# First projections of a decoder block: PSUM tiles that leave are summed over four K tiles, and low parts of weights stand behind the modulation sums in VectorE's order

## The chip, the cores and the metric

The kernel runs on one core of one Trainium2 chip. The metric is the device time of one execution in microseconds (us); the median of three runs before the change is 3016.16 us. TensorE is PE in the profile, VectorE DVE, ScalarE ACT, GpSimd POOL, and SyncE, which issues most DMAs, SP.

## The reference, cut to what matters

```python
D_MODEL = 2048; SEQ = 512            # one sequence, one layer
mod = c_act @ w_ada + b_ada          # c_act = silu(c): one row of 2048; w_ada: 2048 x 12288
sh1, sc1, gt1, sh2, sc2, gt2 = jnp.split(mod, 6, axis=-1)
h = modulate(rms_norm(x, g_mix), sh1, sc1)        # h * (1 + sc1) + sh1
z = h @ w_in
(q_sb, k_sb, v_sb, q_ds, k_ds, v_ds, q_ix, k_ix, w_ix,
 gate_sb, gate_ds) = split_columns(z)
...                                  # two attention branches, gates, w_out, a conv-gated FFN, a final norm
```

All is float32. The kernel computes a float32 product as three products of rounded parts: a factor a is split into a high part (ScalarE rounds it) and a low part (a minus the high part, on VectorE), and high x high, high x low and low x high are summed in PSUM.

## The kernel before, in words

The change lies in the first stage, from about 23 to 246 us. The rows of h are 16 K tiles of 128. Tile d of h needs columns d of the vectors sh1 and sc1, and each of these is a sum over all 2048 rows of w_ada, so that 4 MB of w_ada have to pass before two tiles of h can be made. The 16 K tiles are therefore taken in nine groups (`GR`, L45: one tile, seven times two, one). While PE multiplies group g with the weights, VectorE sums the columns of w_ada for group g + 1 and beyond.

**The modulation sums.** `first_ada` (L682) is a generator; one step is one item: 256 KB of w_ada, loaded by `first_load` (L288, SP) up to ten items ahead. In a group of two tiles there are 16 items, each one row block of 128 x 512. Nearly all are added by VectorE into one accumulator (L697 the first, L699 the others, each reads the accumulator that the one before wrote). In the groups after the second, two of the 16 go to PE instead (L679, `ON_PE`). When the items are through, `hidden` (L707) lets PE sum the accumulator over its partitions (L679 with a vector of ones), VectorE writes the vectors (L716 `modv`, L718 `smix`), and ScalarE makes two instructions per tile: the high part of h (L723) and the whole value (L729). `hidden_rest_` (L736) makes the low part on VectorE (L739).

**The products.** In each group four weight loads ("units") are used, in the order `ORD`: 512 columns of the indexer's queries, the 80 columns of the indexer's keys and weights, 512 more columns of the queries, and 512 columns of the first heads' q and k. A unit's K tiles are those of its group. Of the 13 PSUM tiles, five stay in PSUM through all nine groups (the queries 0, 1, 4, 5 and "kw"). The other eight leave after each group: `evac` (L750) copies the tile to SBUF on ScalarE (L752), and from the second group on VectorE adds it to what is there (L756).

**The order.** The order of the instructions on each engine is written out by hand: it is the order in which the Python code emits them. A unit is one entry of `steps`; before a unit runs, `ahead` (L233) loads weights up to five units on (four buffers) and calls `convert` (L219) for the unit two further on: ScalarE rounds (L229), VectorE subtracts (L230), at once. Then `first_go` (L758) emits the products of each PSUM tile, and after each tile `paced` (L785) emits up to three items of the modulation sums, towards a goal that runs ten items (`LEAD`) ahead of the next group; the goal is held at the end of the next group's sums until `hidden` of that group has been emitted. `hidden` of the next group stands before the third of the four units, `hidden_rest_` before the fourth. After each unit VectorE may get two products `xr` (L670, x times the row factor), and SP a spill of x to HBM.

Of the kernel before, what the change touches and what calls it, by code (L numbers as in the profile page):

```python
# [11 lines left out]
F32 = mybir.dt.float32  # L12
# [17 lines left out]
C_QSB, C_KSB, C_VSB = 0, 1024, 2048  # L30
C_QDS, C_KDS, C_VDS = 3072, 4096, 5120
C_QIX, C_KIX, C_GSB, C_GDS = 6144, 7168, 7248, 9296
# [6 lines left out]
AHEAD = 20  # L39
LEAD = 10  # L40
AHEAD = 10
OF = 2
SP0 = 22
ORD = (0,2,1,3)
GR = (1,2,2,2,2,2,2,2,1)  # L45
PLAIN = 4
DELAY = 3
# [40 lines left out]
SC0 = 4  # L88
LS = 8
L0 = 1  # L90
OF2 = 1
BY_DMA = 14


# [11 lines left out]
def block_kernel(ctx, tc, x, c, w_ada, b_ada, g_mix, w_in, w_o_sb, w_o_dsa, w_out, rel_bias,  # L106
                 g_ffn, w_gate, w_up, conv_w, conv_b, w_down, g_final, buckets, out, dbg=None):
    nc = tc.nc
    x, w_ada, w_in, w_o_sb, w_o_dsa, w_out = x[0], w_ada[0], w_in[0], w_o_sb[0], w_o_dsa[0], w_out[0]
# [18 lines left out]
    def ps():  # L128
        return psum.tile([128, 512], F32, tag="ps", name="ps")
# [11 lines left out]
    def U(w, k0, nk, c0, nn, fn, early=False):  # L141
        steps.append(((w, k0, nk, c0, nn, early), fn))
        units.append(steps[-1][0])
# [9 lines left out]
    def F(fn):  # L153
        steps.append((None, fn))
# [19 lines left out]
    def seven_blocks(r, spec):  # L174
# [3 lines left out]
        return (r.rearrange("p (q b c) -> p q b c", q=q, b=7),  # L178
                w[128 * k0:128 * (k0 + nk), c0:c0 + nn].rearrange("(q k p) (u c) -> p q k u c", q=q, p=128, u=2))

    def is_seven(spec):
        return isinstance(spec[5], str)

    def load(spec):
        w, k0, nk, c0, nn, kind = spec
# [16 lines left out]
    def loaded_sums(r, spec):  # L202

        if spec[5] == "seven by dma":
            b, wb = seven_blocks(r, spec)
            for u in range(2):
                nc.gpsimd.dma_start(b[:, :, 2 + u], wb[:, :, u, 1 - u], accum_op=OP.add)  # L207

    def sums_of(r, spec):

        if not is_seven(spec):
            return
        b, _ = seven_blocks(r, spec)
        if spec[5] == "seven":
            nc.vector.tensor_add(b[:, :, 2:4], b[:, :, 5:7], b[:, :, 0:1].to_broadcast([128, 2, 2, 128]))  # L215
        nc.vector.tensor_add(b[:, :, 1], b[:, :, 3], b[:, :, 5])  # L216
        nc.vector.tensor_add(b[:, :, 0], b[:, :, 4], b[:, :, 1])  # L217

    def convert(r, spec):  # L219

        nn, kind = spec[4], spec[5]
        h = wsp.tile([128, 1792], F32R, tag="wh", name="wh")
        l = wsp.tile([128, 1792], F32R, tag="wl", name="wl")
        if is_seven(spec):
            nc.scalar.copy(h, r)  # L225
            nc.vector.tensor_sub(l, r, h.bitcast(F32))  # L226
            return tuple(v.rearrange("p (q b c) -> p q b c", q=spec[2] // 2, b=7) for v in (h, l))
        h, l = h[:, 0:r.shape[1]], l[:, 0:r.shape[1]]
        nc.scalar.copy(h, r)  # L229
        (nc.gpsimd if kind else nc.vector).tensor_sub(l, r, h.bitcast(F32))  # L230
        return h.rearrange("p (k n) -> p k n", n=nn), l.rearrange("p (k n) -> p k n", n=nn)

    def ahead():  # L233

        def loads(n):
            while len(raws) < min(n, len(units)):
                raws.append(load(units[len(raws)]))

        def sums(n):
            while len(summed_) < min(n, len(units)):  # L240
                k = len(summed_)
                sums_of(raws[k], units[k])
                summed_.append(k)

        while len(parts) < min(at[0] + 3, len(units)):
            n = len(parts)
            loads(n + 4)
            while len(added_) < min(n + 3, len(units)):
                loaded_sums(raws[len(added_)], units[len(added_)])
                added_.append(True)  # L250
            sums(n + 2)
            parts.append(convert(raws[n], units[n]))
            raws[n] = None
# [28 lines left out]
    GROUPS = [(sum(GR[:i]), sum(GR[:i + 1])) for i in range(len(GR))]  # L282
# [424 lines left out]
    def hidden(k0, k1):  # L707

        while not fin:
            advance(back)  # L710
        p, acc, first = fin.pop(0)
        while late:
            evac(*late.pop())
        n = k1 - k0
        on_pe(p, acc, ones[:, 0:1], first, True)
        nc.vector.tensor_add(modv2[:, :, k0:k1], p[:, 0:2 * n].rearrange("p (v a) -> p v a", v=2),  # L716
                             vecs[:, 0:2 * KT].rearrange("p (v a) -> p v a", v=2)[:, :, k0:k1])
        nc.vector.scalar_tensor_tensor(smix[:, k0:k1], modv[:, SC1 * KT + k0:SC1 * KT + k1], 1.0,  # L718
                                       vecs[:, 96 + k0:96 + k1], op0=OP.add, op1=OP.mult)
        for d in range(k0, k1):  # L720
            s, b = smix[:, d:d + 1], modv[:, SH1 * KT + d:SH1 * KT + d + 1]
            h, l, u = T(F32R), T(F32R), xr[d]
            nc.scalar.activation(h, u, AF.Identity, scale=s, bias=b)  # L723
            if d == 0:
                y = T()
                nc.vector.tensor_scalar(y, u, s, b, op0=OP.mult, op1=OP.add)
                u = y
            else:
                nc.scalar.activation(u, u, AF.Identity, scale=s, bias=b)  # L729
            rest.append((l, u, h))  # L730
            xr[d] = None
            hT.append((h, l))
# [3 lines left out]
    def hidden_rest_():  # L736
        while rest:
            l, u, h = rest.pop(0)
            nc.vector.tensor_sub(l, u, h.bitcast(F32))  # L739

    FIRST = [(C_QIX, 512, [(2, 256, 128, False), (3, 384, 128, False), (0, 0, 128, True), (1, 128, 128, True)]),
             (C_QIX + 512, 512, [(6, 256, 128, False), (7, 384, 128, False), (4, 0, 128, True), (5, 128, 128, True)]),
             (C_KIX, 80, [("kw", 0, 80, True)]),
             ((C_QSB, C_KSB), 512, [("q0", 0, 128, False), ("q1", 128, 128, False), ("k0", 256, 128, False), ("k1", 384, 128, False)])]
    part, late = {}, []
    FIRST = [FIRST[i] for i in ORD]

    def evac(key, p, gi, w):  # L750
        t = T()
        nc.scalar.copy(t[0:w, :], p)  # L752
        if gi == 0:
            part[key] = t
        else:
            nc.vector.tensor_add(part[key], part[key], t)  # L756

    def first_go(h, l, gi, tiles):  # L758
        k0, k1 = GROUPS[gi]
        for key, off, w, stay in tiles:  # L760
            if not stay:
                p = ps()[0:w, :]
            elif gi == 0:
                p = part[key] = ps()[0:w, :]
            else:
                p = part[key]
            for k in range(k0, k1):
                mm3(p, h[:, k - k0, off:off + w], l[:, k - k0, off:off + w], *hT[k],
                    k == 0 if stay else k == k0, k == KT - 1 if stay else k == k1 - 1)
            if late:  # L770
                evac(*late.pop())
            if not stay:
                late.append((key, p, gi, w))
            paced(gi)

    def spill(d1):

        for d in range(len(xT_d), min(d1, len(xr))):
            xT_d.append(dram.tile([128, 512], F32, name=f"xT{d}"))
            nc.sync.dma_start(xT_d[d], xT[d])  # L780
            xT[d] = None

    steps_of = {}

    def paced(gi):  # L785

        if gi + 1 == len(GROUPS):
            return
        steps_of[gi] = steps_of.get(gi, 0) + 1
        goal = base[gi + 1] + LEAD + steps_of[gi] * (base[gi + 2] - base[gi + 1]) // sum(len(f[2]) for f in FIRST)  # L790
        if len(hT) < GROUPS[gi + 1][1]:
            goal = min(goal, base[gi + 2])
        for _ in range(3):
            if seen[0] < min(goal, base[-1]):
                advance(back)

    base = [sum(16 // (2 // (b - a)) for a, b in GROUPS[:g]) for g in range(len(GROUPS) + 1)]

    def start():
        nonlocal rate  # L800
        rate[0] = 0
        while len(raws) < 3:
            raws.append(load(units[len(raws)]))
        first_load(16)
        first_norm()
        scaled(1)
        back.append(first_ada())
        while not fin:
            advance(back)
        ahead()  # L810
        hidden(*GROUPS[0])
        hidden_rest_()

    F(start)
    for gi, (k0, k1) in enumerate(GROUPS):
        for i, (c0, nn, tiles) in enumerate(FIRST):
            if i == len(FIRST) - OF and gi + 1 < len(GROUPS):
                F(lambda g=gi + 1: hidden(*GROUPS[g]))
            if i == len(FIRST) - OF2:
                F(hidden_rest_)  # L820
            U(w_in, k0, k1 - k0, c0, nn, lambda h, l, gi=gi, tiles=tiles: first_go(h, l, gi, tiles))
            F(lambda d=k1 + 4: scaled(d))
            F(lambda d=4 * gi + i - SP0: spill(d))

    def first_end():
        rate[0] = 1
# [958 lines left out]
```

## Time and profile before

| | |
|---|---|
| median of the runs (lowest, highest) | 3016.16 us (3015.74, 3017.46) |
| the profiled execution: time, span | 3015.27 us, 3013.6 us |
| PE busy | 2879.1 us (96%) |
| DVE busy | 2449.6 us (81%) |
| ACT busy | 1276.8 us (42%) |
| granted clock of PE, mean of the span | 0.976 |
| the same in slices 1 to 4 (75 us each) | 0.7, 0.8, above 0.9, above 0.9 |

The page cuts the span into 40 slices of 75 us. PE is below nine tenths busy in the first slice, and its clock is below full in the first two; from the third slice to the last it is nearly always at nine tenths or more. A view by windows gives the busy time of each engine in a stretch (PE twice: products and weight loads), its granted clock and the share of the DMA engines; the timeline gives the instructions in order with start and duration and, in brackets, the idle time before them and what ended it.

### The profile page before, as it was taken

Reading aid. Unit: us, or ns where it says so; the run is one execution under the profiler, and the core shown is the slowest. Engines: PE = TensorE matmul, PEld = TensorE weight load, DVE = VectorE, ACT = ScalarE, POOL = GpSimd, SP = SyncE. Lnnn points to the kernel's source line nnn. Section 1 sums busy time; section 2 is a strip of 40 time slices with the busy share of each in tenths; the row PEclk is TensorE's granted clock in tenths of the full one; section 3 lists DMA queues with packets and bytes.
Section 4 is the critical chain, followed back from the end, with each engine's and each line's share of the span. In section 5 each row is a group of like instructions: output and inputs, shape, how many; then the busy total and the mean of one; then the engine's idle time right before and its main releaser. Section 6 shows DMA issues by size and latency. Waiting matters only on the chain.

```text
span 3013.6 us, 53120 instructions
## 1 busy us (share of the span) xinstructions
PE 2879.1 (96%) x20287; PEld 2706.0 (90%) x20287; DVE 2449.6 (81%) x3621; ACT 1276.8 (42%) x1580; POOL 480.6 (16%) x484
## 2 busy tenths in 40 slices
PE   6999999999999999999998999999999999989987
PEld 5778889888888999888998999999999998989986
DVE  6777888888878877459999998888877778786788
ACT  4445433333335444224455444444444445454545
POOL 0000222200112000000123000000044442333330
PEclk7899999999999999999998999999999999999998
DMA  9664247777763445543452434344499888888996
GB/s 289 220 186 146 74 136 231 238 254 251 260 203 102 129 138 168 182 143 113 152 196 85 124 115 120 113 116 124 129 195 194 181 204 207 217 217 187 224 233 212
DMA packets 543855, 527.97 MB, mean 175 GB/s; under 512 B 40943, under 2 KB 444015, under 8 KB 543599
## 3 DMA queue, kind: packets, MB, share of 16 engines
q1 hardware_dynamic: 480303, 471.60, 50.8%
q0 software_dynamic: 56384, 40.39, 9.7%
q10 hardware_dynamic: 6912, 12.59, 1.1%
q8 instruction: 158, 2.59, 0.4%
q14 instruction: 98, 0.80, 0.1%
HBM read 475.12 MB, written 51.92 MB: 175 GB/s over the span
## 4 chain that ended last, share of the span: by engine, by line
PE 66%; DVE 17%; DMA 10%; issue 3%; ACT 2%; SPq 1%; POOL 1%; ACTq 0%; DVEq 0%; POOLq 0%
PE ps L335 21%; PE ps L336 21%; PE ps L337 21%; DVE wl L226 6%; DMA raw<-in_w_down_dram 6%; DMA raw<-in_w_up_dram 1%; DVE raw L216 1%; DVE slot L418 1%; PE ps L679 1%; DVE slot L1634 1%; PE ps L958 1%; ACT wh L225 1%; DVE raw L215 1%; SPq L190 1%; DMA slot<-in_w_ada_dram 1%
## 5 line engine op out<-in xcount | busy, mean ns | idle before, releaser
L336 PE MATMUL ps<-slot,wh 128*128 128x256 f32 (+2 forms) x4624 | 1433.2, 310 | 20.4 <-DVE slot L413 17.7
L337 PE MATMUL ps<-slot,wl 128*128 128x256 f32 (+2 forms) x4624 | 1432.1, 310 | 16.7 <-DVE wl L226 16.6
L335 PE MATMUL ps<-slot,wh 128*128 128x256 f32 (+2 forms) x4624 | 1438.0, 311 | 2.9 <-ACT slot L723 1.4
L336 PEld LDWEIGHTS ps<-slot,wh 128*128 128x128 f32 (+1 forms) x4624 | 892.3, 193 | 65.3 <-DVE slot L413 19.4
L337 PEld LDWEIGHTS ps<-slot,wl 128*128 128x128 f32 (+1 forms) x4624 | 891.8, 193 | 63.8 <-DVE wl L226 19.7
L335 PEld LDWEIGHTS ps<-slot,wh 128*128 128x128 f32 (+1 forms) x4624 | 892.2, 193 | 49.8 <-ACT slot L752 4.5
L225 ACT CAST wh<-raw 128x1792 fp32r<-128x1792 f32 x338 | 570.6, 1694 | 622.0 <-DVE raw L217 207.4
L226 DVE TENSOR_TENSOR wl<-raw,wh 128x1792 fp32r<-128x1792 f32 x338 | 682.2, 2019 | 68.0 <-ACT wh L225 67.6
L336 PE MATMUL ps<-wl,slot 128*128 128x256 f32 (+1 forms) x1708 | 497.1, 291 | 25.9 <-DVE wl L226 25.7
L335 PE MATMUL ps<-wh,slot 128*128 128x256 f32 (+1 forms) x1708 | 497.4, 291 | 11.9 <-ACT slot L468 7.6
L337 PE MATMUL ps<-wh,slot 128*128 128x256 f32 (+1 forms) x1708 | 495.4, 290 | 4.3 <-DVE slot L515 4.3
L336 PEld LDWEIGHTS ps<-wl,slot 128*128 128x128 f32 x1708 | 333.6, 195 | 32.6 <-DVE wl L226 29.5
L335 PEld LDWEIGHTS ps<-wh,slot 128*128 128x128 f32 x1708 | 333.6, 195 | 17.2 <-ACT slot L468 9.0
L337 PEld LDWEIGHTS ps<-wh,slot 128*128 128x128 f32 x1708 | 333.5, 195 | 8.1 <-DVE slot L515 5.9
L229 ACT CAST wh<-raw 128x1024 fp32r<-128x1024 f32 (+3 forms) x178 | 177.6, 998 | 237.1 <-PE ps L336 174.0
L230 DVE TENSOR_TENSOR wl<-raw,wh 128x1024 fp32r<-128x1024 f32 (+3 forms) x178 | 208.4, 1172 | 82.3 <-ACT wh L229 80.2
L216 DVE TENSOR_TENSOR raw<-raw 128x256 f32<-128x256 f32 x338 | 150.4, 445 | 148.2 <-DMA raw<-in_w_down_dram 90.7
L546 DVE SCALAR_TENSOR_TENSOR slot<-slot,c_act 128x512 f32<-128x512 f32 x240 | 193.7, 807 | 6.8
L207 POOL DMA_DIRECT2D raw<-in_w_down_dram x164 | 145.7, 1042 | 266.2 <-DMA raw<-in_w_down_dram 134.7
L207 POOL DMA_DIRECT2D raw<-in_w_gate_dram x56 | 68.8, 1471 | 641.7 <-DVE wl L226 558.2
L217 DVE TENSOR_TENSOR raw<-raw 128x256 f32<-128x256 f32 x338 | 154.7, 458 | 11.6
L215 DVE TENSOR_TENSOR raw<-raw 128x512 f32<-128x512 f32 x200 | 139.2, 696 | 0.0
(226 smaller groups left out, 2327.0 us busy)
## 6 DMA issues: line engine op xcount, KB each, us to landing
slot<-in_w_ada_dram SPq DMA_DIRECT2D x368, 256.0 KB, 4.7
raw<-in_w_in_dram SPq DMA_DIRECT2D x118, 512.0 KB, 5.0
raw<-in_w_down_dram SPq DMA_DIRECT2D x246, 128.0 KB, 4.1
raw<-in_w_gate_dram SPq DMA_DIRECT2D x204, 128.0 KB, 2.8
raw<-in_w_up_dram SPq DMA_DIRECT2D x204, 128.0 KB, 2.8
raw<-in_w_gate_dram SPq DMA_DIRECT2D x88, 256.0 KB, 3.2
raw<-in_w_up_dram SPq DMA_DIRECT2D x88, 256.0 KB, 3.3
raw<-in_w_down_dram SPq DMA_DIRECT2D x82, 256.0 KB, 4.8
```

Source lines behind the costliest of these rows:

```text
L207: nc.gpsimd.dma_start(b[:, :, 2 + u], wb[:, :, u, 1 - u], accum_op=OP.add)
L215: nc.vector.tensor_add(b[:, :, 2:4], b[:, :, 5:7], b[:, :, 0:1].to_broadcast([128, 2, 2, 128]))
L216: nc.vector.tensor_add(b[:, :, 1], b[:, :, 3], b[:, :, 5])
L217: nc.vector.tensor_add(b[:, :, 0], b[:, :, 4], b[:, :, 1])
L225: nc.scalar.copy(h, r)
L226: nc.vector.tensor_sub(l, r, h.bitcast(F32))
L229: nc.scalar.copy(h, r)
L230: (nc.gpsimd if kind else nc.vector).tensor_sub(l, r, h.bitcast(F32))
L335: nc.tensor.matmul(o, lhsT=sh, rhs=mh, start=start, stop=False, skip_group_check=skip)
L336: nc.tensor.matmul(o, lhsT=sh, rhs=ml, start=False, stop=False, skip_group_check=skip)
L337: nc.tensor.matmul(o, lhsT=sl, rhs=mh, start=False, stop=stop, skip_group_check=skip)
L546: nc.vector.scalar_tensor_tensor(acc, raw[n], s, acc, op0=OP.mult, op1=OP.add)
```

## The change

- The nine groups get their own lists of units. First come the five tiles that stay: one unit with four tiles (two loads of 256 columns) and the unit "kw", with the group's own K tiles. Then, in the groups between the first and the last, only one half of the leaving tiles: in even places of the list (counted from 0) the four tiles of the queries (`ix_rest`), in odd ones those of q and k (`qk_first`). From the third group on a half runs over four K tiles, its own group's and those of the group before, as two units of 256 columns by four K tiles, two PSUM tiles each; in the second group it is one unit over two K tiles. In the first group and the last both halves run, over the K tiles that are left.
- A tile that leaves is so copied and added once for four K tiles: 44 copies for 72, and 36 additions for 64. The products are the same 624 (and as many units, 36).
- The low part of a weight unit is not emitted in `convert`, but kept in a list that `low_parts` empties after the first PSUM tile of the running unit, behind the items that `paced` emits there. In the last group only its first unit is treated so.
- `hidden` of the next group stands before the last unit of a group (before: the third of four), and `hidden_rest_` comes behind the first PSUM tile of that unit.
- `paced` counts K tiles times PSUM tiles, and may emit up to n + 1 items after a tile, n being the K tiles of the unit (before: three).

```diff
-OF = 2
-ORD = (0,2,1,3)
...
+    lows = []
+
+    def low_parts():
+
+        while lows:
+            lows.pop(0)()
...
-        (nc.gpsimd if kind else nc.vector).tensor_sub(l, r, h.bitcast(F32))
+        if kind == "low later":
+            lows.append(lambda: nc.vector.tensor_sub(l, r, h.bitcast(F32)))
+        else:
+            nc.vector.tensor_sub(l, r, h.bitcast(F32))
...
+    def ix_stay(k0, k1):
+        return [((C_QIX, C_QIX + 512), 512, k0, k1, [(0, 0, 128, True), (1, 128, 128, True), (4, 256, 128, True), (5, 384, 128, True)]),
+                (C_KIX, 80, k0, k1, [("kw", 0, 80, True)])]
+
+    def ix_rest(k0, k1):
+        return [((C_QIX + 256, C_QIX + 768), 512, k0, k1, [(n, 128 * i, 128, False) for i, n in enumerate((2, 3, 6, 7))])] if k1 - k0 < 3 else \
+               [(C_QIX + 128 * n, 256, k0, k1, [(n, 0, 128, False), (n + 1, 128, 128, False)]) for n in (2, 6)]
+
+    def qk_first(k0, k1):
+        return [((C_QSB, C_KSB), 512, k0, k1, [(n, 128 * i, 128, False) for i, n in enumerate(("q0", "q1", "k0", "k1"))])] if k1 - k0 < 3 else \
+               [(c, 256, k0, k1, [(n + "0", 0, 128, False), (n + "1", 128, 128, False)]) for c, n in ((C_QSB, "q"), (C_KSB, "k"))]
+
+    FIRST = []
+    upto = {ix_rest: 0, qk_first: 0}
+    for gi, (k0, k1) in enumerate(GROUPS):
+        us = ix_stay(k0, k1)
+        for n, f in enumerate((ix_rest, qk_first)):
+            if gi in (0, len(GROUPS) - 1) or gi % 2 == n:
+                us += f(upto[f], k1)
+                upto[f] = k1
+        FIRST.append(us)
...
-            paced(gi)
+                late.append((key, p, k0 == 0, w))
+            paced(gi, k1 - k0)
+            low_parts()
+            if end:
+                hidden_rest_()
...
-        for _ in range(3):
+        for _ in range(n + 1):
             if seen[0] < min(goal, base[-1]):
                 advance(back)
...
     for gi, (k0, k1) in enumerate(GROUPS):
-        for i, (c0, nn, tiles) in enumerate(FIRST):
-            if i == len(FIRST) - OF and gi + 1 < len(GROUPS):
+        for i, (c0, nn, ka, kb, tiles) in enumerate(FIRST[gi]):
+            end = i == len(FIRST[gi]) - 1
+            if end and gi + 1 < len(GROUPS):
                 F(lambda g=gi + 1: hidden(*GROUPS[g]))
-            if i == len(FIRST) - OF2:
-                F(hidden_rest_)
-            U(w_in, k0, k1 - k0, c0, nn, lambda h, l, gi=gi, tiles=tiles: first_go(h, l, gi, tiles))
+            U(w_in, ka, kb - ka, c0, nn, lambda h, l, gi=gi, ka=ka, kb=kb, tiles=tiles, end=end: first_go(h, l, gi, ka, kb, tiles, end),
+              "low later" if (gi, i) < (len(GROUPS) - 1, 1) else False)
```

## Rows read from the trace of the kernel before

**Rows 1.** Windows: length, busy (instructions) PE, PEld, DVE, ACT, POOL, clock, DMA, GB/s
```profile
32.50:48.00 15.50, 6.03 (x15) 4.04 (x15) 15.00 (x22) 1.79 (x3) 0.00 (x0) 0.61 1.09 356
...
48.00:225.00 177.00, 158.35 (x682) 125.82 (x683) 134.16 (x214) 76.55 (x112) 0.00 (x0) 0.90 0.69 215
225.00:246.00 21.00, 21.00 (x98) 17.36 (x97) 14.70 (x24) 13.12 (x22) 0.00 (x0) 1.00 0.74 212
```

**Rows 2.** Waits from 48 to 247 us: total us, times, longest
```profile
DVE wl L230 <- ACT wh L229: 33.3, 12, 4.3
...
PE ps L679 <- DVE slot L699: 27.8, 7, 9.9
```

**Rows 3.** Groups of VectorE's instructions from 48 to 247 us
```profile
L699 DVE SCALAR_TENSOR_TENSOR slot<-slot,c_act 128x512 f32<-128x512 f32 x79 | 58.9, 746 | 0.8
L756 DVE TENSOR_TENSOR slot<-slot 128x512 f32<-128x512 f32 x64 | 43.0, 684 | 2.6 <-ACT slot L752 2.6
```

**Rows 4.** Timeline of VectorE in one group: start, duration
```profile
127.95 0.17 DVE L716 TENSOR_TENSOR modv<-ps,vecs 128x4 f32<-128x4 f32 x1 [1.96 <-PE ps L679]
...
132.53 1.23 DVE L230 TENSOR_TENSOR wl<-raw,wh 128x1024 fp32r<-128x1024 f32 x1 [4.21 <-ACT wh L229]
133.67 0.48 DVE L697 TENSOR_SCALAR slot<-slot,c_act 128x512 f32<-128x512 f32 x1
134.07 0.68 DVE L756 TENSOR_TENSOR slot<-slot 128x512 f32<-128x512 f32 x1
134.67 0.74 DVE L699 SCALAR_TENSOR_TENSOR slot<-slot,c_act 128x512 f32<-128x512 f32 x1
...
135.94 1.52 DVE L699 SCALAR_TENSOR_TENSOR slot<-slot,c_act 128x512 f32<-128x512 f32 x2
137.38 1.28 DVE L739 TENSOR_TENSOR slot<-slot 128x512 fp32r<-128x512 f32 x2
```

**Rows 5.** Timeline of PE around the same place
```profile
119.35 0.95 PE L679 MATMUL ps<-c_act,slot 128*128 128x1 f32 x8
120.16 0.49 PE L335 MATMUL ps<-slot,wh 128*128 128x512 f32 x1
...
126.05 1.87 PE L679 MATMUL ps<-ones,slot 128*128 128x1 f32 x8 [2.86 <-DVE slot L699]
127.77 0.77 PE L335 MATMUL ps<-slot,wh 128*128 128x512 f32 x1
...
132.19 0.63 PE L336 MATMUL ps<-slot,wh 128*128 128x512 f32 x1
...
138.67 0.39 PE L335 MATMUL ps<-slot,wh 128*128 128x512 f32 x1
...
143.21 0.39 PE L337 MATMUL ps<-slot,wl 128*128 128x512 f32 x1
```

**Rows 6.** Timeline of ScalarE at the same place
```profile
128.35 0.81 ACT L723 ACTIVATE slot<-slot,modv,smix 128x512 fp32r<-128x512 f32 x1 [5.64 <-DVE smix L718]
...
131.47 1.03 ACT L229 CAST wh<-raw 128x1024 fp32r<-128x1024 f32 x1
```

**Rows 7.** Timeline of VectorE: the vectors of groups 1, 2 and 3
```profile
50.28 0.16 DVE L716 TENSOR_TENSOR modv<-ps,vecs 128x4 f32<-128x4 f32 x1 [2.02 <-PE ps L679]
...
74.16 0.17 DVE L716 TENSOR_TENSOR modv<-ps,vecs 128x4 f32<-128x4 f32 x1 [1.96 <-PE ps L679]
...
101.02 0.16 DVE L716 TENSOR_TENSOR modv<-ps,vecs 128x4 f32<-128x4 f32 x1 [1.96 <-PE ps L679]
```

**Rows 8.** Line 716 in the whole span: the vectors of all nine groups
```profile
L716 DVE TENSOR_TENSOR modv<-ps,vecs x9: 151/163/166, 31.2 to 226.8; 128x4 f32<-128x4 f32 x7, 128x2 f32<-128x2 f32 x2
```

**Rows 9.** DMA from 48 to 225 us, and SP's longest wait from 22 to 247 us
```profile
q1 hardware_dynamic: 38665, 38.00, 68.7%
...
slot<-in_w_ada_dram SPq DMA_DIRECT2D x86, 256.0 KB, 4.5
...
SPq L198 <- DVE wl L230: 52.5, 18, 4.7
```

More of the change, by code (lines that the diff above doesn't have):

```diff
@@ L90 @@
 L0 = 1
-OF2 = 1
 BY_DMA = 14
@@ L179, in seven_blocks @@
                 w[128 * k0:128 * (k0 + nk), c0:c0 + nn].rearrange("(q k p) (u c) -> p q k u c", q=q, p=128, u=2))
+    lows = []
+    def low_parts():
+        while lows:
+            lows.pop(0)()
     def is_seven(spec):
-        return isinstance(spec[5], str)
+        return isinstance(spec[5], str) and spec[5][0:5] == "seven"
     def load(spec):
@@ L739, in hidden_rest_, with evac @@
             nc.vector.tensor_sub(l, u, h.bitcast(F32))
[L743 to L746, printed above, removed]
+    def ix_stay(k0, k1):
[16 more added lines that the diff above has]
+        FIRST.append(us)
     part, late = {}, []
-    FIRST = [FIRST[i] for i in ORD]
-    def evac(key, p, gi, w):
+    def evac(key, p, first, w):
         t = T()
         nc.scalar.copy(t[0:w, :], p)
-        if gi == 0:
+        if first:
             part[key] = t
@@ L756, in evac, with first_go @@
             nc.vector.tensor_add(part[key], part[key], t)
-    def first_go(h, l, gi, tiles):
-        k0, k1 = GROUPS[gi]
+    def first_go(h, l, gi, k0, k1, tiles, end):
         for key, off, w, stay in tiles:
@@ L762, in first_go @@
                 p = ps()[0:w, :]
-            elif gi == 0:
+            elif k0 == 0:
                 p = part[key] = ps()[0:w, :]
@@ L772, in first_go @@
             if not stay:
-                late.append((key, p, gi, w))
-            paced(gi)
+                late.append((key, p, k0 == 0, w))
[3 more added lines that the diff above has]
+                hidden_rest_()
     def spill(d1):
@@ L783, in block_kernel, with paced @@
     steps_of = {}
-    def paced(gi):
+    def paced(gi, n):
         if gi + 1 == len(GROUPS):
             return
-        steps_of[gi] = steps_of.get(gi, 0) + 1
-        goal = base[gi + 1] + LEAD + steps_of[gi] * (base[gi + 2] - base[gi + 1]) // sum(len(f[2]) for f in FIRST)
+        steps_of[gi] = steps_of.get(gi, 0) + n
+        goal = base[gi + 1] + LEAD + steps_of[gi] * (base[gi + 2] - base[gi + 1]) // sum((f[3] - f[2]) * len(f[4]) for f in FIRST[gi])
         if len(hT) < GROUPS[gi + 1][1]:
             goal = min(goal, base[gi + 2])
-        for _ in range(3):
+        for _ in range(n + 1):
             if seen[0] < min(goal, base[-1]):
@@ L810, in start @@
         ahead()
+        low_parts()
         hidden(*GROUPS[0])
@@ L814, in block_kernel @@
     F(start)
+    spilled = 0
     for gi, (k0, k1) in enumerate(GROUPS):
-        for i, (c0, nn, tiles) in enumerate(FIRST):
-            if i == len(FIRST) - OF and gi + 1 < len(GROUPS):
+        for i, (c0, nn, ka, kb, tiles) in enumerate(FIRST[gi]):
+            end = i == len(FIRST[gi]) - 1
+            if end and gi + 1 < len(GROUPS):
                 F(lambda g=gi + 1: hidden(*GROUPS[g]))
-            if i == len(FIRST) - OF2:
-                F(hidden_rest_)
-            U(w_in, k0, k1 - k0, c0, nn, lambda h, l, gi=gi, tiles=tiles: first_go(h, l, gi, tiles))
+            U(w_in, ka, kb - ka, c0, nn, lambda h, l, gi=gi, ka=ka, kb=kb, tiles=tiles, end=end: first_go(h, l, gi, ka, kb, tiles, end),
+              "low later" if (gi, i) < (len(GROUPS) - 1, 1) else False)
             F(lambda d=k1 + 4: scaled(d))
-            F(lambda d=4 * gi + i - SP0: spill(d))
+            F(lambda d=spilled - SP0: spill(d))
+            spilled += 1
     def first_end():
```

## The prediction, made before the changed kernel ran

> **What bounds the kernel now.** I read the page first. Over the span PE is the bound: 96% busy, and at full clock from the third slice on, so that time saved ahead of that moves the end by the same amount. The exception is the first 246 us, so I cut these into windows [rows 1]. From 48 to 225 us PE is busy for 158 of 177 us at a clock of 0.90; from 225 us on it is full, at 1.00. The view of waits says for whom PE stands there: for the modulation sums on VectorE, 27.8 us in 7 waits [rows 2]. VectorE is not full either (134 of 177 us), and what it waits for is ScalarE's rounding of weights, 33.3 us. Those two waits are one loop, and the timelines show it. PE finishes its units and waits 2.86 us at 126.05 for the last modulation sum [rows 5]; the vectors are written at 127.95; VectorE's next instruction is a low part of weights, which needs a rounding that stands on ScalarE behind four instructions for h, 128.35 to 131.47 [rows 6]; VectorE idles 4.21 us until 132.53 [rows 4], and all sums for the next group stand behind that. So the sums are late again one group on. PE pays twice: after its wait the products come 0.44 us apart (127.77 to 132.19, ten steps), against 0.227 (138.67 to 143.21, twenty steps) [rows 5], which is 1.2 against 2.4 GHz; some 12 products per group run so, 12 x 0.21 = 2.5 us. A group lasts 26.9 us (74.16 to 101.02, 101.02 to 127.95) [rows 4, 7]. This is the stage that the change touches.
>
> **VectorE per group, before and after.** I take durations from start to start. A sum is 0.67 between other work (134.67, 0.74 long, to the next start, as 134.07 plus 0.60 puts it) and 0.76 where sums follow each other (135.94, two in 1.52); the first is 0.40; an addition of a leaving tile 0.60 (134.07 to 134.67); a low part of 1024 columns 1.14 (132.53 to 133.67); a low part of h, or an `xr`, 0.60 (137.38, two in 1.28, which overlap) [rows 4]. The low part of "kw" and the two vectors I put at 0.3 and 0.4, by the 0.17 of L716. Before: 14 sums 9.1, eight additions 4.8, three low parts and "kw" 3.7, two `xr` and two low parts of h 2.4, vectors 0.4: 20.4, plus the idle 4.2 and 2.0 (before L716): 26.6, against 26.9 measured, so the sum holds. After: four additions fewer per group on the average, 2.4 us (28 of the 64 go in all [rows 3]); but the sums now run in bursts of five, at 0.76, so 10.3 for 9.1. Work 19.2. The 4.2 wait becomes smaller: behind the vectors now come up to five items (four on VectorE: 0.40 + 3 x 0.76 = 2.7), and only then the low part of "kw", whose rounding is ready 0.4 + 0.2 + 3.1 (the four ScalarE instructions) + 0.3 = 4.0 after the vectors. So about 0.9 to 1.2 of it is left. VectorE needs 20.4.
>
> **PE per group.** 78 products at 0.227 make 17.7; two items on PE at 0.81 each (119.35 to 120.16) 1.6; the sum over partitions 0.9 (half the 1.72 from 126.05 to 127.77, which ran at the low clock) [rows 5]. Together 20.2, if it never waits and stays at 2.4 GHz. Both engines so come to some 20.4, and I take 21.0, which allows 0.6 for waits of either for the other.
>
> **Does the order allow it?** In a group now follow the unit S (four staying tiles, 24 products, 5.5 us), K (6, 1.4), R1 and R2 (24 each, 5.5). The goal of `paced` reaches the end of the next group's sums in K; so VectorE's last sum is emitted one whole unit, R1, before `hidden`. Counted from the vectors: four sums to 3.1, low part of K at 4.0, low parts of h to 5.5, one addition and five sums to 10.0, an addition, a sum and the low part of R1 to 12.5 (PE starts R1 at about 13.5), two sums and two `xr` to 15.2, two sums to 16.8, then low parts of R2 and of the next S to 19.1, two additions to 20.5. PE wants the accumulator at 19.0, the end of R1: there it is 2.2 early. The price of the later `hidden`: before, 48 products covered the way from the vectors to the new h, now 24, that is 5.5 us. The low part of the first new tile is there at 4.9 and wanted at about 5.6, that of the second at 5.5 against 6.3. These covers of 0.7 to 0.8 us are the thinnest in the plan; if one is gone, PE waits what is missing, once per group.
>
> **Edits that I put at nothing.** ScalarE loses 28 copies; it idles more than half of the stage, 77 of 177 us busy [rows 1]. PSUM: two leaving tiles, five staying and one for the sums make eight banks, as before; each leaving tile now takes 12 products, 2.7 us, so its copy has longer. DMA: four more DMAs, two of them in the first group ahead of the sums of the second; between nothing and 4 x 4.5 us (the landing of a w_ada load [rows 9]) if each were waited for; I take nothing, because the loads run five units ahead. Of the weights, 4096 rows of 2 KB (two units x 16 K tiles x 128) become 8192 of 1 KB. A packet costs 68.7% x 16 x 177 / 38665 = 0.050 us of one engine [rows 9], so 0 to 4096 x 0.050 / 16 = 12.8 us of all sixteen over the stage, beside 177 x 0.69 = 122 now. The shorter stage (149 us for the 177) raises their share to about 0.82, or 0.90 with the dearer rows: below the 1.09 that 32.5 to 48 us show [rows 1], so it stays hidden; uncovered, all of the 12.8 would show.
>
> The Trainium skill weighs on this point from both sides. Its page "DMA: Bandwidth & Descriptors" (Specifications) asks for no more than 512 bytes for line rate, by which the shorter rows cost nothing. The same page (Anatomy of one DMA) gives each DMA a fixed cost of about 2.0 us, on the other issue path; as an estimate from the page, four more would be 8 us if nothing lay over them, and the gain below would be 22. The trace of before does not show which it is.
>
> **The sum.** Group 1: VectorE alone bounds it (15.0 of 15.5 us busy [rows 1]); ahead of its `hidden` comes one more low part of 1024 columns: 1.1 plus some slower sums, +1.5. Group 2 (23.9 before, 50.28 to 74.16 [rows 7]): VectorE has waiting and vectors 4.0, low parts of K and h 1.5, 12 sums left 9.1, two low parts 2.3, two `xr` 1.2: 18.1, and I take 18.5: -5.4. Group 3 (26.9): PE still waits once and runs 12 products slowly, 20.2 + 2.5 = 22.7: -4.2. Groups 4 to 8, whose vectors came at 226.8 [rows 8], 125.8 after the third's: four at 21.0 and the last, of one tile, whose items on PE and partition sum are half as long, 20.2 - 1.2 + 0.5 = 19.5; 103.5 in all: -22.3. After the last vectors PE has 87 products on either plan: 0. In all 1.5 - 5.4 - 4.2 - 22.3 = -30.4. What follows the stage is full on PE and does not change. So the profiled execution's 3015.27 becomes 2984.9; the median of the runs lies 0.9 above it, which gives 2986.
>
> **Rivals.** (a) *The wait moves to the low parts of h.* For it: the thin cover above, and a ScalarE copy that stands in the way. Against it: a delay of VectorE also delays the next `hidden`. With 1.5 us per group in seven groups: 10.5 of the 30 are lost, 2996. (b) *Nothing is gained*: the stage is bound by its w_ada loads, so that faster sums only meet waits for data. For it: SP waits 52.5 us for low parts before it can issue weight loads [rows 9], and w_ada loads queue behind those. Against it: VectorE's sums stood idle for 0.8 us in all after 48 us [rows 3]. Then 3016, within 6. (c) *Slower, by starvation*: SP's queue is in order; a weight load waits for a low part that now stands behind sums, and the loads of later sums stand behind that weight load. The lookahead is ten items and falls to five as h fills the buffers. If it falls short, VectorE waits a whole landing, 4.5 us, per burst of sums, two bursts a group: 20.4 + 9 = 29.4, 2.5 over the present 26.9; seven groups give +18, 3034. It decides from two landings per group on; one landing still gains some 2 us a group.
>
> **How the numbers follow.** Forecast 0.72, its own range 2976 to 2995 (PE at its 20.2 in each group and no loss in group 1 at one end; 22.2 a group and slow rows at the other); (a) 0.14; (b) 0.05; (c) 0.09. The range that should hold 8 in 10 reaches into (a): 2974 to 3002. What a measurement here can tell from no change is 0.2%, 6 us: faster 0.86, the same 0.06, slower 0.08.
>
> **What would show it.** Right: 28 additions and copies fewer; the vectors of successive groups 20 to 22 us apart; no wait near 4 us of VectorE for a rounding behind the vectors; PE's waits for L699 gone after the third group, its clock near 1.00 from about 75 us on; the stage over near 216 us instead of 246. Wrong: PE waiting for L739 (rival a); VectorE waiting for w_ada (b, c); or a stretch after the stage that grows by what the stage lost.

## The result and the profile after

The changed kernel takes 2980.89 us (median of four runs, 2977.20 to 2984.17); the kernel before, run beside it, 3015.95 (3013.64 to 3017.46). The ratio is 0.9891, with a 95% interval of 0.9878 to 0.9904: 29 to 37 us faster. A second comparison on another chip (below, e10) gives 2979.35 against 3009.24, 29.9 us. The forecast was 2986, with a range of 2974 to 3002.

The profiled execution took 2984.17 us, span 2982.5; 3015.27 and 3013.6 before. PE leaves the stage (its first product for the v heads) at 215.66 us for 245.46: 29.8 of the 31.1 us lie in the stage. Line numbers have moved: the sums are now L706 and on PE L686, the vectors L723, the copies L777 and additions L781, the roundings L233, the low parts L235 (later) and L237 (at once), the instructions for h L730, L736 and L746.

The windows, as in [rows 1]: in the same 177 us, of which the last 9 now belong to the next stage, PE is busy 15 us longer, at a granted clock of 0.95 for 0.90, and the DMA engines' share rises from 0.69 to 0.83.

```profile
48.00:225.00 177.00, 173.45 (x839) 144.01 (x840) 141.13 (x219) 78.93 (x115) 0.00 (x0) 0.95 0.83 256
```

The waits from 22 to 220 us, against [rows 2]. PE's wait for sums has fallen from 27.8 us in seven to one of 5.1, in group 1 (e10, the same kernel, has one more of 1.73 in group 2). VectorE's wait for roundings now stands in two lines, L235 and L237, 19.7 us together for the 33.3 before; the 7.9 of L237 come behind the last vectors, where PE is full. Up to the last vectors it is 11.1 us (from 48 to 196 us) for 29.6 (from 48 to 225). VectorE's wait for PE's sum over partitions, ahead of the vectors, has fallen from 11.9 us in seven to one of 2.0. VectorE's wait for copies has grown from 2.6 us to 11.1: that is VectorE ahead of PE.

```profile
DVE wl L235 <- ACT wh L233: 11.8, 8, 4.3
DVE slot L781 <- ACT slot L777: 11.1, 9, 2.0
DVE wl L237 <- ACT wh L233: 7.9, 5, 1.9
...
PE ps L686 <- DVE slot L706: 5.1, 1, 5.1
...
DVE modv L723 <- PE ps L686: 2.0, 1, 2.0
```

VectorE's groups, against [rows 3]: as many sums, 36 additions for 64.

```profile
L706 DVE SCALAR_TENSOR_TENSOR slot<-slot,c_act 128x512 f32<-128x512 f32 x79 | 59.2, 750 | 1.9
L781 DVE TENSOR_TENSOR slot<-slot 128x512 f32<-128x512 f32 x36 | 24.4, 687 | 11.1 <-ACT slot L777 11.1
```

One group on VectorE, against [rows 4]. Behind the vectors at 132.53 stand four sums; the wait for the rounding is 0.74, not 4.21; the low parts of h start 4.1 us after the vectors. Ahead of the next vectors VectorE waits 0.76 us for the copy of PE's last tile.

```profile
132.53 0.15 DVE L723 TENSOR_TENSOR modv<-ps,vecs 128x4 f32<-128x4 f32 x1
132.72 0.16 DVE L725 SCALAR_TENSOR_TENSOR smix<-modv,vecs 128x2 f32<-128x2 f32 x1
132.80 0.48 DVE L704 TENSOR_SCALAR slot<-slot,c_act 128x512 f32<-128x512 f32 x1
133.32 2.33 DVE L706 SCALAR_TENSOR_TENSOR slot<-slot,c_act 128x512 f32<-128x512 f32 x3
136.39 0.33 DVE L235 TENSOR_TENSOR wl<-raw,wh 128x160 fp32r<-128x160 f32 x1 [0.74 <-ACT wh L233]
136.63 1.29 DVE L746 TENSOR_TENSOR slot<-slot 128x512 fp32r<-128x512 f32 x2
...
152.47 0.69 DVE L781 TENSOR_TENSOR slot<-slot 128x512 f32<-128x512 f32 x1 [0.76 <-ACT slot L777]
153.08 0.16 DVE L723 TENSOR_TENSOR modv<-ps,vecs 128x4 f32<-128x4 f32 x1
```

ScalarE in the same place, against [rows 6]: the four instructions for h still run before the rounding, but the rounding is now that of the small unit.

```profile
132.92 0.82 ACT L730 ACTIVATE slot<-slot,modv,smix 128x512 fp32r<-128x512 f32 x1 [1.03 <-DMA raw<-in_w_in_dram]
...
136.05 0.31 ACT L233 CAST wh<-raw 128x160 fp32r<-128x160 f32 x1
```

PE, against [rows 5]: the sums over partitions start without a wait, and products follow at full pace. After the vectors of group 1 PE stands for more than 0.3 us at two places only: 1.73 us at 72.40 for a copy that frees a PSUM tile (the first row), and 1.33 us at 180.58 for a load (the last).

```profile
72.40 0.63 PE L342 MATMUL ps<-slot,wh 128*128 128x512 f32 x1 [1.73 <-ACT slot L777]
...
131.11 0.95 PE L686 MATMUL ps<-ones,slot 128*128 128x1 f32 x8
...
151.65 0.95 PE L686 MATMUL ps<-ones,slot 128*128 128x1 f32 x8
...
180.58 0.61 PE L686 MATMUL ps<-c_act,slot 128*128 128x1 f32 x4 [1.33 <-DMA slot<-in_w_ada_dram]
```

The vectors of all groups, against [rows 8]: the last at 196.5 for 226.8.

```profile
L723 DVE TENSOR_TENSOR modv<-ps,vecs x9: 152/156/161, 29.9 to 196.5; 128x4 f32<-128x4 f32 x7, 128x2 f32<-128x2 f32 x2
```

The starts of L716 or L723 (L726 in e1), read from the timelines, measure the stage. This table holds them for all kernels. "Steady" is the mean of the four periods from the vectors of group 3 to those of group 7; "last" is the one from group 7 to group 8; "end" is PE's first product of the next stage; the last column is the difference of the medians to the kernel before on the same chip.

| kernel | group 1 | 2 | 3 | steady | last | end | to before |
|---|---|---|---|---|---|---|---|
| before | 50.3 | 74.2 | 101.0 | 26.3 | 20.7 | 245.5 | |
| changed | 50.1 | 68.1 | 91.5 | 20.5 | 22.9 | 215.7 | -35.1 |
| e1, low parts later alone | 48.9 | 70.3 | 94.8 | 24.5 | 19.9 | 232.0 | -13.3 |
| e2, low parts at once | 49.6 | 68.8 | 92.3 | 22.8 | 24.5 | 227.0 | -18.2 |
| e3, vectors a unit earlier | 47.9 | 67.3 | 89.3 | 21.8 | 19.5 | 221.3 | -23.7 |
| e4, 28 idle additions | 48.8 | 66.8 | 91.0 | 22.5 | 20.0 | 219.4 | -25.9 |
| e5, last sums off PE | 49.6 | 67.6 | 90.8 | 20.5 | 19.9 | 212.0 | -33.9 |
| e6, e5 and `xr` later | 48.6 | 67.7 | 92.4 | 20.5 | 19.8 | 213.6 | -28.9 |
| e7, low parts of h late | 49.1 | 68.5 | 95.6 | 25.6 | 22.4 | 239.4 | -5.7 |
| e8, two K tiles | 49.5 | 70.9 | 93.5 | 23.5 | 21.4 | 222.8 | -24.3 |
| e9, e5 and group 1 on PE | 49.1 | 67.1 | 88.9 | 20.5 | 19.9 | 210.1 | -34.7 |
| e10, changed, again | 48.8 | 66.8 | 88.6 | 20.5 | 22.9 | 212.8 | -29.9 |

From the end of the stage to the end of the span the twelve traces take 2758 to 2770 us, and the two of the changed kernel 2766.8 and 2769.1, so differences of some 5 us between kernels are better read from "end" than from the medians. The two traces of the changed kernel themselves end the stage 2.8 us apart.

### The profile page after: what moved, and what is told of

Its sections match the earlier page's. It is cut to its first block, busy times and chain, and to the rows that moved or that the text cites. A ratio compares the mean times of both kernels' runs of the same rounds, so it can differ in the third digit from the quotient of the medians.

```text
span 2982.5 us, 53020 instructions
## 1 busy us (share of the span) xinstructions
PE 2863.6 (96%) x20287; PEld 2696.7 (90%) x20287; DVE 2437.4 (82%) x3593; ACT 1259.9 (42%) x1552; POOL 481.6 (16%) x484
## 4 chain that ended last, share of the span: by engine, by line
PE 64%; DVE 17%; DMA 11%; issue 4%; ACT 2%; SPq 2%; POOL 1%; ACTq 0%; DVEq 0%; POOLq 0%
PE ps L342 20%; PE ps L344 20%; PE ps L343 20%; DVE wl L230 6%; DMA raw<-in_w_down_dram 5%; DMA raw<-in_w_up_dram 1%; DMA slot<-in_w_ada_dram 1%; DVE raw L220 1%; DVE slot L425 1%; DVE slot L1664 1%; DMA raw<-in_w_in_dram 1%; PE ps L988 1%; ACT wh L229 1%; DVE raw L219 1%; DVE slot L553 1%
## 5 line engine op out<-in xcount | busy, mean ns | idle before, releaser
L343 PE MATMUL ps<-slot,wh 128*128 128x256 f32 (+1 forms) x4624 | 1431.9, 310 | 18.9 <-DVE slot L420 15.9
L344 PE MATMUL ps<-slot,wl 128*128 128x256 f32 (+1 forms) x4624 | 1430.5, 309 | 16.1 <-DVE wl L230 16.0
L342 PE MATMUL ps<-slot,wh 128*128 128x256 f32 (+1 forms) x4624 | 1434.2, 310 | 9.7 <-ACT slot L777 4.4
L343 PEld LDWEIGHTS ps<-slot,wh 128*128 128x128 f32 x4624 | 890.6, 193 | 64.4 <-DVE slot L420 17.7
L344 PEld LDWEIGHTS ps<-slot,wl 128*128 128x128 f32 x4624 | 890.6, 193 | 62.2 <-DVE wl L230 18.7
L342 PEld LDWEIGHTS ps<-slot,wh 128*128 128x128 f32 x4624 | 890.6, 193 | 53.3 <-ACT slot L777 5.4
L342 PE MATMUL ps<-wh,slot 128*128 128x256 f32 (+1 forms) x1708 | 496.6, 291 | 13.3 <-ACT slot L475 8.9
L233 ACT CAST wh<-raw 128x1024 fp32r<-128x1024 f32 (+3 forms) x178 | 177.6, 999 | 263.8 <-PE ps L343 191.3
L237 DVE TENSOR_TENSOR wl<-raw,wh 128x1024 fp32r<-128x1024 f32 (+2 forms) x146 | 179.4, 1230 | 54.9 <-ACT wh L233 53.7
L211 POOL DMA_DIRECT2D raw<-in_w_gate_dram x56 | 68.5, 1448 | 642.1 <-DMA raw<-in_w_gate_dram 584.5
```

The source lines that it names most:

```text
L342: nc.tensor.matmul(o, lhsT=sh, rhs=mh, start=start, stop=False, skip_group_check=skip)
L343: nc.tensor.matmul(o, lhsT=sh, rhs=ml, start=False, stop=False, skip_group_check=skip)
L344: nc.tensor.matmul(o, lhsT=sl, rhs=mh, start=False, stop=stop, skip_group_check=skip)
```

## The experiments

Theory: the gain is a loop of waits that is broken (late sums, PE's wait, four instructions for h ahead of a rounding, VectorE held behind that); PE is the bound after. Rival: the gain is the work taken off VectorE, 28 additions and their copies.

**e1: only the low parts later.** The kernel before with `low_parts`, nothing else.

```diff
+        if kind == "low later":
+            lows.append(lambda: nc.vector.tensor_sub(l, r, h.bitcast(F32)))
...
             paced(gi)
+            low_parts()
```

> Only the low parts of weights are moved behind the modulation sums; unit lists, the 64 additions, 72 copies and the place of the vectors stay as before the change. Theory (the gain is the loop of waits, broken): VectorE's wait for the rounding behind the vectors falls from 4.2 us to about 1.9 (up to three sums and an addition now stand in it), the wait of 2.0 before the vectors and all 20.4 us of work stay: 24.3 us per group for 26.6, so about -16 us: 3000, first stage over near 230 us. Rival (the gain is the 28 additions and copies that are gone): no change, 3016 within 6.

Measured: 2998.43 us (before 3011.76; ratio 0.9960, 0.9946 to 0.9974), 24.5 us per group. With all 64 additions in place 13 us are won, so work is not the whole. But the way was not the one expected: only one sum got in front of the low part, and the wait for the rounding is still 3.81 us. That the period came out as forecast (24.3) is luck.

```profile
119.57 0.17 DVE L726 TENSOR_TENSOR modv<-ps,vecs 128x4 f32<-128x4 f32 x1 [0.19 <-PE ps L689]
119.77 0.17 DVE L728 SCALAR_TENSOR_TENSOR smix<-modv,vecs 128x2 f32<-128x2 f32 x1
119.85 0.49 DVE L707 TENSOR_SCALAR slot<-slot,c_act 128x512 f32<-128x512 f32 x1
124.16 1.23 DVE L238 TENSOR_TENSOR wl<-raw,wh 128x1024 fp32r<-128x1024 f32 x1 [3.81 <-ACT wh L236]
```

What went is the other wait, ahead of the vectors: 0.19 us for the 1.96 of [rows 4]. A low part now stands there behind the last sum, and fills the time in which PE sums the accumulator. PE still waits for sums in each group, 1.84 us at 118.30: the loop is shorter here, not broken.

**e2: low parts at once, all else changed.**

```diff
-              "low later" if (gi, i) < (len(GROUPS) - 1, 1) else False)
+              False)
```

> The changed kernel with the low parts of weights emitted at once, as before the change; sums over four K tiles, unit lists and places of the vectors as changed. Theory (loop): the rounding of the next unit stands on ScalarE behind the four instructions for h, so VectorE waits about 3.6 us behind the vectors again, sums and low parts of h come behind that, and PE waits some 2.7 us for the low part of the first new tile: 23 to 24.5 us per group, 2992 to 3000. Rival (count of VectorE instructions): as many as in the changed kernel, so 2981 within 6.

Measured: 2993.56 us (0.9939, 0.9923 to 0.9955), 22.8 us per group. VectorE executes as many instructions as in the changed kernel, and the gain is 18 us for 30: the rival falls. The waits from 50 to 200 us are those of the theory: the roundings again, up to 3.5 us each, and PE for the low part of the new h.

```profile
DVE wl L237 <- ACT wh L233: 24.5, 7, 3.5
...
PE ps L343 <- DVE slot L746: 9.2, 5, 2.5
```

**e3: the vectors one unit earlier.**

```diff
-            if end and gi + 1 < len(GROUPS):
+            if i == len(FIRST[gi]) - 2 and gi + 1 < len(GROUPS):
```

> The changed kernel with the vectors and the high parts of h emitted before the last but one unit of a group instead of before the last. Theory: VectorE's last sum comes at about the middle of the third unit, so PE waits some 2.6 us per group for it and then runs about 12 products at 1.2 GHz: 24 to 25.5 us per group for 20.5, five to six groups: 3000 to 3010. Rival (more products cover the way from the vectors to the new tiles of h, nothing lost): 2981 or a little less.

Measured: 2988.04 us (0.9925, 0.9908 to 0.9942), 21.8 us per group: slower than the changed kernel by some 6 us, where 19 to 29 were expected. VectorE, not PE, pays most: behind the vectors it waits for the rounding of a large unit again, 3.82 us in group 1 and 3.04 in the steady groups, where the changed kernel waits 0.75 for a small one (the waits from 50 to 200 us, and PE's for sums). The longest of PE's waits in that window, 4.5 us, is ahead of the vectors of group 3; in the groups at 110.6 and 132.4 us it is 0.27 and 1.09 us, and after these the products keep the full pace, so the slow products that I had added did not come.

```profile
DVE wl L235 <- ACT wh L233: 23.4, 8, 3.8
...
PE ps L686 <- DVE slot L706: 7.9, 6, 4.5
```

**e4: 28 additions put back, into a tile that nobody reads.**

```diff
             nc.vector.tensor_add(part[key], part[key], t)
+            if more:
+                nc.vector.tensor_add(t, t, part[key])
```

> The changed kernel with 28 more additions of 128x512 on VectorE, one behind each addition of a tile summed over three or four K tiles (into a tile that nobody reads), so that VectorE has the 64 additions of before in the order of the change. Theory (loop; PE is the bound now at 20.5 us per group): VectorE idles 0.76 us per group ahead of the vectors and has 4 x 0.6 more to do, so a group grows by about 1.6: +9 us, 2990. Rival (count): the saving of 28 x 0.6 goes, and with it the most of the gain: 2998 or more.

Measured: 2985.91 us (0.9914, 0.9898 to 0.9931). A steady group takes 22.5 us for 20.5 (expected 22.1), but the stage ends only 4 to 7 us later than in the two traces of the changed kernel, because the last period falls from 22.9 to 20.0 us. With the additions of before in the order of the change, the stage is still 26 us shorter than before, 23 without that luck in the last period. VectorE is the bound here: its additions stand wall to wall up to the vectors, and its one wait left is 0.75 us per group for the small rounding.

```profile
134.32 0.69 DVE L783 TENSOR_TENSOR slot<-slot 128x512 f32<-128x512 f32 x1
134.93 0.68 DVE L781 TENSOR_TENSOR slot<-slot 128x512 f32<-128x512 f32 x1
135.65 0.69 DVE L783 TENSOR_TENSOR slot<-slot 128x512 f32<-128x512 f32 x1
136.25 0.15 DVE L723 TENSOR_TENSOR modv<-ps,vecs 128x4 f32<-128x4 f32 x1
```

**e5: the last group's sums all on VectorE.** This goes after the wait at 180.58.

```diff
-                if k + i < PK if k0 == 0 else k0 > 1 and (k + i) % 8 in ON_PE:
+                if k + i < PK if k0 == 0 else 1 < k0 < KT - 1 and (k + i) % 8 in ON_PE:
```

> The changed kernel with the last group's sums all on VectorE (the two items on PE of that group move to VectorE, 2 x 0.5 us). Theory: in the changed kernel PE waits 1.33 us at 180.58 for the w_ada load of such an item and then runs slowly for some 12 products; VectorE has idle time there. So -1.3 -2.3 -0.8: the last period falls from 22.9 to about 18.8 us, the whole by about 4 against the changed kernel. Rival: the load is late for VectorE instead and PE waits for that: no difference to the changed kernel.

Measured: 2975.29 us (0.9888, 0.9869 to 0.9907; before 3009.18), the last period 19.9 us for 22.9, the stage over at 212.0. So that period lost 3 us to the item on PE, near the 4 expected: PE still waits there, for the low part of h, but 0.84 us only.

```profile
179.14 0.50 PE L343 MATMUL ps<-slot,wh 128*128 128x512 f32 x1 [0.84 <-DVE slot L746]
```

**e6: e5, and two products `xr` out of group 1.**

```diff
-            F(lambda d=k1 + 4: scaled(d))
+            F(lambda d=k1 + (2 if k1 == 1 else 4): scaled(d))
```

> As e5, and two of the four products of x and the row factor that stand among the sums of group 1 are emitted one group later. Theory: VectorE alone bounds group 1, so its vectors come 1.2 us earlier, and about 1 us of that stays against e5. Rival: group 2 is bound by VectorE too and gives it back: as e5.

Measured: 2980.31 us (0.9899, 0.9881 to 0.9917). The vectors of group 1 come 1.1 us earlier than in e5 (48.55 for 49.63), those of group 2 no longer (67.74 for 67.62): group 2 gives it back, as the rival had it. Group 3 then starts 1.6 us later than in e5. There PE waits 2.8 us for copies where in e5 it waits 1.8; but that period is 23.4 and 21.8 us in the two traces of the changed kernel alone, so I do not count it.

**e7: the low parts of h behind the last tile of the unit.**

```diff
-            if end:
+            if end and key == tiles[-1][0]:
                 hidden_rest_()
```

> The changed kernel with the low parts of the new tiles of h emitted behind the last PSUM tile of the last unit instead of behind the first. Theory (the cover of the low parts is 0.7 to 0.8 us): they come an addition and up to five sums later, about 4.4 us, so PE waits some 3.7 us per group at the next unit and runs slowly after: 24 to 26 us per group for 20.5, the whole 20 to 35 us over the changed kernel. Rival (there is room enough, or VectorE waited for PE anyway): within 6 us of the changed kernel.

Measured: 3003.44 us (0.9973, 0.9961 to 0.9986), 25.6 us per group: 24 us of the 30 are gone, from one place in VectorE's queue. PE's waits for L746 from 50 to 215 us, and one of them:

```profile
PE ps L343 <- DVE slot L746: 19.4, 7, 3.6
```
```profile
105.14 0.50 PE L343 MATMUL ps<-slot,wh 128*128 128x512 f32 x1 [3.25 <-DVE slot L746]
```

**e8: leaving tiles over two K tiles, the rest changed.**

```diff
-            if gi in (0, len(GROUPS) - 1) or gi % 2 == n:
-                us += f(upto[f], k1)
-                upto[f] = k1
+            us += f(k0, k1)
```

> The changed kernel with the leaving tiles summed over two K tiles in each group, as before the change (units: staying tiles, kw, four query tiles, four of q and k; 64 additions, 72 copies); low parts later and vectors before the last unit, as changed. Theory: only the four additions per group come back, as with the 28 idle additions (22.6 us per group): VectorE 21.6 us of work and a wait of about 1: 22 to 22.8 us per group, the stage over near 220 us, 10 us over the changed kernel. Rival (the four K tiles are needed for the order too: shorter tiles give the copies no time and PE waits for PSUM): 24 us per group or more, 20 us over.

Measured: 2984.84 us (0.9917, 0.9902 to 0.9932), 23.5 us per group, between theory (22 to 22.8) and rival (24). The mechanism is the rival's: in each of six groups PE waits for the copy of a short tile. At 121.20 it waits 1.16 us, the copy stands on ScalarE behind the four instructions for h, and eight products some 0.43 us apart follow (granted clock 0.55 from 121.2 to 125.0); 20.5 + 1.2 + 8 x 0.2 = 23.3 is the whole period. VectorE idles 2.2 us in such a group, so the additions do not set it, though by e4 they alone would make 22.5. The end of the stage is less late than the period says, since 24 products less are left after the last vectors. The four K tiles are worth 7 to 10 us by the end of the stage, 6 to 11 by the medians.

```profile
PE ps L342 <- ACT slot L775: 9.3, 7, 2.0
```
```profile
120.58 1.06 ACT L775 COPY slot<-ps 128x512 f32<-128x512 f32 x2
```
```profile
121.20 0.57 PE L342 MATMUL ps<-slot,wh 128*128 128x512 f32 x1 [1.16 <-ACT slot L775]
```

**e9: e5, and two sums of group 1 on PE.**

```diff
-                if k + i < PK if k0 == 0 else k0 > 1 and (k + i) % 8 in ON_PE:
+                if k + i < PK if k0 == 0 else 1 <= k0 < KT - 1 and (k + i) % 8 in ON_PE:
```

> As e5 (the last group's sums all on VectorE), and two of the 16 sums of group 1 on PE, which waits 5.1 us there. Theory: VectorE alone bounds group 1, two sums at 0.76 less make its vectors 1.5 us earlier, and nothing is moved into group 2: -1.5 against e5, -5 against the changed kernel, the stage over near 210.5 us. Rival: PE at 1.2 GHz takes 1.87 us per item and becomes the bound there, or the copies that stood behind the vectors of group 2 cost what is won: as e5.

Measured: 2974.55 us (five runs, 2970.89 to 2975.99; 0.9879, 0.9864 to 0.9895), the stage over at 210.1, expected 210.5. Group 1 gains 0.5 us of the 1.5, for PE now waits 3.63 us there for the load of its item.

```profile
42.91 1.87 PE L686 MATMUL ps<-c_act,slot 128*128 128x1 f32 x8 [3.63 <-DMA slot<-in_w_ada_dram]
```

**e10: the changed kernel beside e9.** No edit.

> The changed kernel itself, beside e9 on one chip. The stage was 29.8 us shorter in its trace, the median of the first runs 35 lower. Theory (the whole gain lies in the first stage): 30 to 31 us under the kernel before. Rival (some 4 us come from later stages): 34 to 35 under.

Measured: 2979.35 us (five runs, 2975.57 to 2983.64; 0.9897, 0.9882 to 0.9913), 29.9 under the kernel before. The interval (26 to 36 us) holds both the theory and the rival, so the median alone does not part them. The traces speak for the theory: of the 31.1 us between the spans of the first two 29.8 lie in the stage, and from the stage's end on the changed kernel takes 2766.8 and 2769.1 us, the kernel before 2768.1. e9 is 4.8 us below e10 on the same chip, with the lowest median of all; its slowest run and the fastest of e10 touch, so the 4.8 is less sure than the stage ends, 2.8 us apart here.

## Why the prediction was right, step by step

- **What bounds the stage**: right. Late sums and the wait for the rounding were one loop. The low parts later (e1, -13.3) and all else (e2, -18.2) nearly add up to the whole. The parts do not act as planned by themselves: e1 removes the wait ahead of the vectors and leaves the one for the rounding. From e1 to e8, which adds the order of the units, the later vectors and the pacing, the stage ends 9 us earlier, and from e8 to the changed kernel, which adds the four K tiles, 7 to 10. Of the order, the vectors and the pacing only the vectors were tried singly (e3).
- **VectorE per group**, 19.2 us of work and a wait of 0.9 to 1.2: from 112.00 to 132.53 it idles 0.75 and 0.76 us and so works 19.0. The wait for the rounding was 0.75. The one wait near 4 us that is left, 4.26 us at 189.30, is not behind the vectors; without the item on PE (e5) it is 0.58.
- **PE per group**, 20.2, taken as 21.0: the four steady periods are 20.53 to 20.55, and PE is busy for 100.0 of the 100 us from 75 to 175. The 0.6 us that I had allowed for waits of either for the other were not needed; that it is 20.5 and not 20.2 is the products, 18.1 us for 78 (0.232 each, taken as 0.227). So PE is the bound, VectorE close behind: 2.4 us more on VectorE in e4 make the group 2.0 longer.
- **The order**: the low parts of h were done 5.3 us after the vectors (predicted 5.5). Their cover was mis-sized: PE wants the first at 138.68, and it is done at about 137.3, so 1.4 us and not 0.7. The plan had left out the item on PE (0.81 us) that stands in that unit, at 134.78. That there is no more room than that is shown by e7: moved back by an addition and five sums, they cost 24 us. The later place of the vectors is worth 6 to 8 us by the end of the stage (e3), most of it because a small rounding and not a large one then stands behind them.
- **The sum, group by group**: group 1 +1.5: its period grew by 1.0 (19.1 to 20.1), but it started 1.2 us earlier (first vectors at 29.9 for 31.2), so its vectors come 0.2 earlier; group 2 18.5, measured 18.0; group 3 22.7, measured 23.4 and in e10 21.8; four groups at 21.0, measured 20.5. In group 3 PE did wait once, but for a copy (1.73 us at 72.40, and eight slow products); the half of the group before runs over two K tiles, as in e8. In e10 this wait is 0.27 us, and no slow products follow. The last period was mis-sized: 19.5, measured 22.9 in both traces of the changed kernel. There PE stood 1.33 us for a w_ada load and then ran eight products slowly; e5 takes the item away, and the period is 19.9. It is a late load, as in rival (c), but not by (c)'s way: from 165 to 178 us, when these loads were issued, SP waited at most 0.6 us at a time and 0.3 for a low part; the DMA engines' share from 174 to 180 us was 1.06. Why the load was late is not shown. After the last vectors PE took 0.5 us more than before. In all -29.8 for -30.4; that the sum is so close is in part luck, for 3.4 us too little in the last period, 0.7 in group 3 and 0.5 behind the last vectors stand against 1.8 too much in the four groups, 1.7 in group 1 and 0.5 in group 2.
- **Edits put at nothing**: the stage after did not change (from its first product to the end 2768.1 us before, 2766.8 after). The DMA share was expected at 0.82 to 0.90 over the 149 us that are left: it is 0.86 from 48 to 197 us. The shorter rows: over the whole span the main queue has 4160 packets more, and its packets took 0.508 x 16 x 3013.6 = 24495 us of single engines before and 0.515 x 16 x 2982.5 = 24576 after. These 81 us more say nothing: the same product is 24285 in e10, the changed kernel again, and 24152 in e1, which has the packets of before. A price cannot be told from zero; PE, at least, waits for no load in the steady groups. Before, after, and after again (e10):

```profile
q1 hardware_dynamic: 480303, 471.60, 50.8%
```
```profile
q1 hardware_dynamic: 484463, 471.60, 51.5%
```
```profile
q1 hardware_dynamic: 484463, 471.60, 50.9%
```

- **Four more DMAs** cost nothing to be seen: the stage is 29.8 us shorter. The gain is not the 22 us that the fixed cost from the Trainium skill's page "DMA: Bandwidth & Descriptors" (Anatomy of one DMA, for the other issue path) would have left as an estimate. The line-rate rule of the same page of the Trainium skill (Specifications, 512 bytes) is not contradicted: no price of the shorter rows can be seen.
- **The median** came out 5 us under the forecast. The profiled execution, 2984.17, is 0.7 from the 2984.9 that the sum gave; the four runs of the changed kernel lie 7 us apart, and the profiled one was the slowest of them.

## What to carry to other kernels

When one engine waits for a second and the second for a third, look for an instruction that only stands in a queue's way: here a low part that is wanted two units later held up sums that are wanted next. The order was worth more than the work: with all the additions put back, 26 of some 30 us stayed. What the longer sums over K are worth is order too: with short ones PE waits for a copy that stands behind other work (e8). And after such a cure look at the covers that are left, by the place in the queue that can least move; low parts of h that came one PSUM tile later took 24 us back.

## What the runs showed that was not expected

- When PE falls to 1.2 GHz. The wait of 1.33 us at 180.58 was followed by three products 0.23 to 0.31 us apart and then eight at about 0.43; the granted clock from 180 to 186 us is 0.72, and 1.00 from 186 to 192. The length of the wait does not decide it: behind waits of 1.16 and 1.15 us in e8 (at 121.20 and 144.65) there are eight slow products, behind 1.85 us in e8 (75.27), 2.62 in e1 (167.62) and 2.25 in the kernel before (205.10) none. So a price of 12 slow products per wait, as the prediction took it, holds for most waits of the kernel before (9 to 13) and not for each. What decides it was not tried.
- A slower VectorE can give some of its time back: in e4 the groups are longer, the same item on PE finds its load in time, and the last period is 2.9 us shorter than in the changed kernel.
- Loads are near in the early groups. From 49 to 67 us the DMA engines' share in e9 is 1.10, at 345 GB/s (1.09 at 356 GB/s from 32.5 to 48 us before the change), and in group 1 moving sums to PE exchanges a wait for sums for one for loads (3.63 us at 42.91). Group 2 is still bound by VectorE: two products `xr` more there (e6) lengthen it by their own 1.2 us.

```profile
180.00:186.00 6.00, 5.42 (x19) 4.37 (x20) 4.76 (x8) 1.54 (x3) 0.00 (x0) 0.72 0.27 94
186.00:192.00 6.00, 6.00 (x28) 4.68 (x27) 1.82 (x2) 1.68 (x2) 0.00 (x0) 1.00 0.48 117
```
```profile
49.00:67.00 18.00, 15.99 (x71) 12.25 (x71) 15.19 (x23) 7.40 (x11) 0.00 (x0) 0.88 1.10 345
```
